# Row normalisation by absolute sums: whole 48 KB packets, a held load, and a one-row lead of the first store

## The chip, the core and the metric

The kernel runs on one core of one Trainium2 chip. The metric is device time in microseconds, the median of several executions. A second source is the profile: one execution recorded by the hardware profiler, with its own span from the first to the last instruction.

The engines that matter are VectorE (DVE in the profile), ScalarE (ACT), SyncE (SP) and the 16 DMA engines that move data between the main memory (HBM) and the on-chip buffer (SBUF). A DMA is issued by an instruction in the queue of SyncE (loads here; the profile calls the DMA queue q1) or of ScalarE (stores here; q10). Instructions of one queue run in their order, and each may first wait for semaphores, which other instructions or finished DMAs raise.

## The reference

```python
x: (32, 512, 1024) float32

def reference(x):
    sums = np.sum(np.abs(x), axis=-1, keepdims=True)
    return (x / (sums + 1e-8)).astype(np.float32)
```

There are 16,384 rows of 1,024 numbers, 4 KB each: 67.11 MB are read and 67.11 MB written. Each row is divided by the sum of its absolute values.

## The kernel before

The rows are cut into 11 tiles. Each of the 128 partitions holds 12 rows of a tile (48 KB a partition, 6,144 KB a tile), except in the last tile, which has 8 rows. `HEAD = 32` rows of a partition make up tiles 0, 1 and the last; within a partition the rows of a tile are contiguous in HBM, so a load or store may move up to 48 KB in one piece.

Four buffers of 48 KB a partition hold the tiles (`sbuf`, `BUFS = 4`): the pool gives out a buffer each time a tile is requested, and a fifth request gets the first buffer back, once all that used it is done. A tile is loaded by `load(i)` (line 87, SyncE's queue), worked on in place by `compute(i)`, and written by `store(i)` (line 97, ScalarE's queue). So the load of tile i + 4 waits for the store of tile i to have landed.

`compute(i)` calls `normalize`, which runs on VectorE: line 47 sums the absolute values of each row (a reduction over the tile), line 54 adds 1e-8, line 56 takes the reciprocal (the row factors `inv`), line 58 multiplies the first `kv` rows by their factors, and line 65 does `kt` rows one at a time. The remaining `ks` rows are scaled by ScalarE in line 68. `split` gives `(kt, ks)`: (3, 4) for tile 0, (0, 3) for tiles 1 and 2, (0, 2) for tile 9 and (4, 4) for tile 10; all others are scaled by VectorE alone.

`max_dma_last_dim` sets the piece, called a packet here, in which a DMA moves a partition's rows. Each of the 16 DMA engines serves 8 partitions. Before, tiles 0 and 1 are loaded in packets of 48 KB (`WHOLE`) and the others of 24 KB (`HALF`; the last tile's come to 16 KB). The store of tile 0 is in two parts: 3 rows in packets of 4 KB, then 9 rows in packets of 36 KB. Tile 8 is stored by two DMAs of 6 rows, tiles 9 and 10 in whole packets, the others in 24 KB packets.

The schedule is by hand (`manual_schedule`): each engine's queue has its instructions in the order in which the code calls them. The calls are load(0) to load(3), then compute(0), store(0), load(4), compute(1), store(1), load(5) and so on.

Of the kernel before, what the change touches and what calls it, by code (L numbers as in the profile page):

```python
# [1 line left out]

# [4 lines left out]

FP32 = mybir.dt.float32
EPS = 1e-8


@with_exitstack
def kernel(
    ctx: ExitStack,
    tc: tile.TileContext,
    x: bass.AP,
    out: bass.AP,
):
    nc = tc.nc
    P = nc.NUM_PARTITIONS  # L20

    x_flat = x.flatten_outer_dims()
    out_flat = out.flatten_outer_dims()
    n, d = x_flat.shape

    R = 12
    BUFS = 4
    HEAD = 32
    per_partition = n // P
    assert n % P == 0 and (per_partition - HEAD) % R == 0  # L30
    rows = [R] * ((per_partition - HEAD) // R + 2) + [HEAD - 2 * R]

    def piece(flat, i):
        head = flat[: P * HEAD, :].rearrange("(p r) d -> p r d", p=P)
        if i < 2:
            return head[:, R * i : R * (i + 1), :]
        if i == len(rows) - 1:
            return head[:, 2 * R :, :]
        a = P * (HEAD + R * (i - 2))
        return flat[a : a + P * R, :].rearrange("(p r) d -> p r d", p=P)  # L40

    sbuf = ctx.enter_context(tc.tile_pool(name="sbuf", bufs=BUFS))
    stats = ctx.enter_context(tc.tile_pool(name="stats", bufs=len(rows)))

    def normalize(x_tile, k, kv, kt):
        s = stats.tile([P, R], FP32)
        nc.vector.tensor_reduce(  # L47
            out=s[:, :k],
            in_=x_tile[:, :k, :],
            axis=mybir.AxisListType.X,  # L50
            op=mybir.AluOpType.add,
            apply_absolute_value=True,
        )
        nc.vector.tensor_scalar_add(out=s[:, :k], in0=s[:, :k], scalar1=EPS)  # L54
        inv = stats.tile([P, R], FP32)
        nc.vector.reciprocal(out=inv[:, :k], in_=s[:, :k])  # L56
        if kv:
            nc.vector.tensor_mul(  # L58
                out=x_tile[:, :kv, :],
                in0=x_tile[:, :kv, :],  # L60
                in1=inv[:, :kv].unsqueeze(2).to_broadcast([P, kv, d]),
            )
        for r in range(kv, kv + kt):
            row = x_tile[:, r, :]
            nc.vector.tensor_scalar_mul(out=row, in0=row, scalar1=inv[:, r : r + 1])  # L65
        for r in range(kv + kt, k):
            row = x_tile[:, r, :]
            nc.scalar.activation(  # L68
                out=row,
                in_=row,  # L70
                func=mybir.ActivationFunctionType.Copy,
                scale=inv[:, r : r + 1],
            )

    last = len(rows) - 1
    split = {0: (3, 4), 1: (0, 3), 2: (0, 3), last - 1: (0, 2), last: (4, 4)}

    tiles = {}

    HALF, WHOLE = 24576, 49152
    FIRST = 3

    def load(i):
        x_tile = tiles[i] = sbuf.tile([P, R, d], FP32, name="x_tile")
        nc.sync.dma_start(out=x_tile[:, : rows[i], :], in_=piece(x_flat, i), max_dma_last_dim=WHOLE if i < 2 else HALF)  # L87

    def store(i):
        if i == 0:  # L90
            parts = [(0, FIRST, 4 * d), (FIRST, R, WHOLE)]
        elif i == last - 2:
            parts = [(0, R // 2, HALF), (R // 2, R, HALF)]
        else:
            parts = [(0, rows[i], WHOLE if i >= last - 1 else HALF)]
        for a, b, size in parts:
            nc.scalar.dma_start(
                out=piece(out_flat, i)[:, a:b, :],
                in_=tiles[i][:, a:b, :],
                max_dma_last_dim=size,  # L100
            )

    def compute(i):
        k = rows[i]
        kt, ks = split.get(i, (0, 0))
        normalize(tiles[i], k, k - kt - ks, kt)

    with tc.manual_schedule():
        for i in range(BUFS):
            load(i)  # L110
        for i in range(len(rows)):
            compute(i)
            store(i)
            if i + BUFS < len(rows):
                load(i + BUFS)


# [1 line left out]
_INS = ['x']  # L119
_OUTS = [((32, 512, 1024), 'float32')]  # L120


# [23 lines left out]
```

## Time and profile before

| what | us |
|---|---|
| median of 3 runs | 316.6 (316.44 to 316.62) |
| span of the profiled execution | 315.2 |
| VectorE busy | 260.6 |
| ScalarE busy | 18.5 |
| VectorE waiting for loads | 29.8, of which 17.8 for the first |
| mean rate of the DMA engines over the span | 426 GB/s |

The profile's times are microseconds from the start of its span. In a line of the timeline the columns are start, duration, engine, line of the code and operation; in the chain of waits they are start, duration and what the chain went through; in the list of waits they are total, number of times, and longest. The lines of the kernel are those of the kernel before.

### The profile page before, as it was taken

The numbers are of one execution on the slowest core, as the hardware profiler recorded it, in microseconds if no ns is written. First come the engines' busy times: TensorE is split into PE (matmuls) and PEld (weight loads), VectorE is DVE, ScalarE is ACT, GpSimd is POOL, SyncE is SP. The second block draws the span as 40 slices with busy tenths as digits, with TensorE's granted clock in tenths as the row PEclk, the third lists the DMA queues.
The fourth block names the chain that finished last, engine by engine and source line by source line (L and its number), as shares of the span: only waits on it lengthen the run. The fifth ranks groups of instructions, "written<-read, shape, count | busy, mean of one in ns | idle before, by whom it ended". The sixth has DMA issues, their size and how long they took to land.

```text
span 315.2 us, 172 instructions
## 1 busy us (share of the span) xinstructions
DVE 260.6 (83%) x50; ACT 18.5 (6%) x17; POOL 0.2 (0%) x4
## 2 busy tenths in 40 slices
DVE  0079999999999999989996997999699969999000
ACT  0010503004000000000000000000000000203200
POOL 0000000000000000000000000000000000000000
DMA  8999999999999999999999999999999999999997
GB/s 318 480 399 412 437 407 464 411 436 413 415 446 437 415 446 437 415 449 434 415 449 437 412 449 437 412 449 437 415 446 437 415 437 434 432 428 496 399 408 324
DMA packets 5761, 134.22 MB, mean 426 GB/s; under 512 B 385, under 2 KB 385, under 8 KB 769
## 3 DMA queue, kind: packets, MB, share of 16 engines
q1 hardware_dynamic: 2736, 67.11, 49.8%
q10 hardware_dynamic: 3024, 67.11, 49.4%
q14 instruction: 1, 0.00, 0.0%
HBM read 67.11 MB, written 67.11 MB: 426 GB/s over the span
## 4 chain that ended last, share of the span: by engine, by line
DVE 40%; DMA 33%; another core or an unknown queue 18%; ACT 1%; issue 0%; SPq 0%
DVE s L47 23%; DMA x_tile<-in_x_dram 17%; DMA out_dram<-x_tile 16%; DVE x_tile L58 15%; ACT x_tile L68 1%; DVE x_tile L65 1%; DVE inv L56 0%; DVE s L54 0%; SPq L87 0%
## 5 line engine op out<-in xcount | busy, mean ns | idle before, releaser
L47 DVE TENSOR_REDUCE s<-x_tile 128x12 f32<-128x12288 f32 (+1 forms) x11 | 138.2, 12562 | 29.8 <-DMA x_tile<-in_x_dram 29.8
L58 DVE TENSOR_TENSOR x_tile<-x_tile,inv 128x12288 f32<-128x12288 f32 (+3 forms) x10 | 113.6, 11358 | 0.5
L68 ACT ACTIVATE x_tile<-x_tile,inv 128x1024 f32<-128x1024 f32 x16 | 17.2, 1138 | 256.9 <-DVE inv L56 256.9
L65 DVE TENSOR_SCALAR x_tile<-x_tile,inv 128x1024 f32<-128x1024 f32 x7 | 4.8, 749 | 0.0
L56 DVE RECIPROCAL inv<-s 128x12 f32<-128x12 f32 (+1 forms) x11 | 2.5, 226 | 0.4
L68 ACT ACT_TABLE_LOAD x1 | 1.3, 1283 | 17.8 <-DMA x_tile<-in_x_dram 17.8
L54 DVE TENSOR_SCALAR s<-s 128x12 f32<-128x12 f32 (+1 forms) x11 | 1.9, 174 | 0.4
L130 POOL MEMSET const-bfloat16-1.0<- 128x1 bf16 x1 | 0.1, 101 | 0.0
L130 POOL MEMSET const-uint8-127<- 128x1 uint8 x1 | 0.1, 101 | 0.0
L130 POOL MEMSET const-float32-0.0<- 128x1 f32 x1 | 0.1, 98 | 0.2 <-issue 0.2
L130 POOL MEMSET const-float32-1.0<- 128x1 f32 x1 | 0.1, 98 | 0.0
## 6 DMA issues: line engine op xcount, KB each, us to landing
x_tile<-in_x_dram SPq DMA_DIRECT2D x10, 6144.0 KB, 36.9
out_dram<-x_tile ACTq DMA_DIRECT2D x8, 6144.0 KB, 49.1
out_dram<-x_tile ACTq DMA_DIRECT2D x2, 3072.0 KB, 33.4
out_dram<-x_tile ACTq DMA_DIRECT2D x1, 4608.0 KB, 37.9
x_tile<-in_x_dram SPq DMA_DIRECT2D x1, 4096.0 KB, 32.2
out_dram<-x_tile ACTq DMA_DIRECT2D x1, 4096.0 KB, 20.9
out_dram<-x_tile ACTq DMA_DIRECT2D x1, 1536.0 KB, 29.3
```

Of the source, the lines that this page charges most:

```text
L47: nc.vector.tensor_reduce(out=s[:, :k], in_=x_tile[:, :k, :], axis=mybir.AxisListType.X, op=mybir.AluOpType.add, apply_absolute_value=True,)
L54: nc.vector.tensor_scalar_add(out=s[:, :k], in0=s[:, :k], scalar1=EPS)
L56: nc.vector.reciprocal(out=inv[:, :k], in_=s[:, :k])
L58: nc.vector.tensor_mul(out=x_tile[:, :kv, :], in0=x_tile[:, :kv, :], in1=inv[:, :kv].unsqueeze(2).to_broadcast([P, kv, d]),)
L65: nc.vector.tensor_scalar_mul(out=row, in0=row, scalar1=inv[:, r : r + 1])
L68: nc.scalar.activation(out=row, in_=row, func=mybir.ActivationFunctionType.Copy, scale=inv[:, r : r + 1],)
L130: nc = _bacc.Bacc("TRN2", target_bir_lowering=False, num_devices=1)
```

## The change

All loads and stores use packets of 48 KB (32 KB for the last tile), except the lead of the first store, which is now one row instead of three; the rest of that store is 11 rows in packets of 44 KB. Tile 8 is stored by one DMA.

Only tiles 0, 1 and 2 are loaded ahead of the loop (`EARLY = 3`). `load(3)` is now called from within `compute(1)`, after line 56 has made the factors of tile 1 and before its rows are multiplied. There, one number in each partition of tile 3's new buffer is first written by VectorE with a copy of a factor (`tensor_copy`, 128 x 1), and the load, which overwrites it, has to come after that copy. The loop itself is as before, with `load(i + BUFS)` at the end of step i.

```diff
-    def normalize(x_tile, k, kv, kt):
+    def normalize(x_tile, k, kv, kt, between):
...
         inv = stats.tile([P, R], FP32)
         nc.vector.reciprocal(out=inv[:, :k], in_=s[:, :k])
+        between(inv)
...
+    PACKET = 49152
+    FIRST = 1
+    EARLY = 3
...
-    HALF, WHOLE = 24576, 49152
-    FIRST = 3
-
-    def load(i):
+    def load(i, after=None):
         x_tile = tiles[i] = sbuf.tile([P, R, d], FP32, name="x_tile")
-        nc.sync.dma_start(out=x_tile[:, : rows[i], :], in_=piece(x_flat, i), max_dma_last_dim=WHOLE if i < 2 else HALF)
+        if after is not None:
+            nc.vector.tensor_copy(out=x_tile[:, 0, 0:1], in_=after[:, 0:1])
+        nc.sync.dma_start(out=x_tile[:, : rows[i], :], in_=piece(x_flat, i), max_dma_last_dim=PACKET)
 
     def store(i):
-        if i == 0:
-            parts = [(0, FIRST, 4 * d), (FIRST, R, WHOLE)]
-        elif i == last - 2:
-            parts = [(0, R // 2, HALF), (R // 2, R, HALF)]
-        else:
-            parts = [(0, rows[i], WHOLE if i >= last - 1 else HALF)]
+        k = rows[i]
+        parts = [(0, FIRST, 4 * d), (FIRST, k, PACKET)] if i == 0 else [(0, k, PACKET)]
...
     def compute(i):
         k = rows[i]
         kt, ks = split.get(i, (0, 0))
-        normalize(tiles[i], k, k - kt - ks, kt)
+
+        def between(inv):
+            if i == 1:
+                load(EARLY, after=inv)
+
+        normalize(tiles[i], k, k - kt - ks, kt, between)
 
     with tc.manual_schedule():
-        for i in range(BUFS):
+        for i in range(EARLY):
             load(i)
         for i in range(len(rows)):
             compute(i)
             store(i)
             if i + BUFS < len(rows):
                 load(i + BUFS)
```

## The prediction

> **What bounds the kernel now.** I read the page first: spans, busy shares, DMA row and queues.
>
> ```profile
> span 315.2 us, 172 instructions
> ...
> DVE 260.6 (83%) x50; ACT 18.5 (6%) x17; POOL 0.2 (0%) x4
> ...
> DMA  8999999999999999999999999999999999999997
> ...
> q1 hardware_dynamic: 2736, 67.11, 49.8%
> q10 hardware_dynamic: 3024, 67.11, 49.4%
> ```
>
> VectorE has 55 us to spare; the DMA engines have none. Their row is full in every slice but the first and last, and the two queues' packets fill 99.2% of the span. The bytes are fixed, so the time falls only if packets get cheaper, and grows by every microsecond in which both queues stand empty. Next, the list of waits of VectorE and of SyncE's queue, and the chain of waits:
>
> ```profile
> DVE s L47 <- DMA x_tile<-in_x_dram: 29.8, 6, 17.8
> ...
> SPq L87 <- DMA out_dram<-x_tile: 242.1, 8, 63.3
> ```
>
> ```profile
> 0.73 17.05 DMA x_tile<-in_x_dram
> ...
> 160.35 0.37 SPq L87
> ...
> 189.48 0.37 SPq L87
> ```
>
> SyncE's loads wait for stores to give buffers back, and one cycle of load and store takes 189.48 - 160.35 = 29.1 us. VectorE waits 29.8 - 17.8 = 12.0 us for later loads, so it has little more slack than that. Last the timeline of tiles 0 to 3, which shows what each engine could do when:
>
> ```profile
> 36.78 2.40 ACTq L97 DMA_DIRECT2D out_dram<-x_tile  x2
> ...
> 51.84 0.23 DVE L56 RECIPROCAL inv<-s 128x12 f32<-128x12 f32 x1
> 52.10 9.76 DVE L58 TENSOR_TENSOR x_tile<-x_tile,inv 128x9216 f32<-128x9216 f32 x1
> ...
> 61.78 12.94 DVE L47 TENSOR_REDUCE s<-x_tile 128x12 f32<-128x12288 f32 x1
> ...
> 84.91 12.94 DVE L47 TENSOR_REDUCE s<-x_tile 128x12 f32<-128x12288 f32 x1
> ...
> 111.23 12.95 DVE L47 TENSOR_REDUCE s<-x_tile 128x12 f32<-128x12288 f32 x1
> ...
> 293.25 0.34 ACTq L97 DMA_DIRECT2D out_dram<-x_tile  x1
> ```
>
> The second part of store 0 (9 rows) goes out at the end of the 2.40 us, near 38.8, and the page's DMA issues give it 37.9 us to land: 76.7. Until then the DMA engines carry four loads and store 0 without a hole. The last store is issued at 293.25 and ends the kernel.
>
> **The order of the loads.** The loop still calls load(4) after store(0), and that is ahead of compute(1), from which load(3) is now called. So the fourth load on SyncE is that of tile 4, not tile 3, and the fourth request to the pool is tile 4's. It takes the free fourth buffer and waits for nothing: four loads still go out at once. Tile 3 is the fifth request; it gets tile 0's buffer. Its `tensor_copy` writes that buffer, so it must wait until both parts of store 0 have read it out. In the built program VectorE's copy, between tile 1's reciprocal and its multiplication, waits for exactly these two DMAs, and SyncE's fifth load for them and for VectorE.
>
> Queued behind the copy on VectorE is everything else: the multiplication of tile 1, hence store 1 on ScalarE's queue, all later stores behind it, and load(5) on SyncE, which needs store 1. What is late next is therefore store 1.
>
> **Edit 1, packets: -1.37 us.** The trace's packet records give 912 ns for 24 KB and 1,815 ns for 48 KB, so one packet more costs 2 x 912 - 1,815 = 9 ns (a 4 KB packet's 159 ns fits: 9 plus a twelfth of 1,806). Packets per engine removed: loads of tiles 2 to 9, 16 to 8 each, 64, and the last tile 8; stores of tiles 1 to 8, 64; store 0, from 24 + 8 to 8 + 8, 16. Together 152 x 9 ns = 1.37 us, all on the DMA engines, which set the end. Bounds: 0 (nothing gained in the mixed stretches) and -1.37. I take the full amount, since the 912 ns are those of the mixed stretches.
>
> The Trainium skill (DMA: Bandwidth & Descriptors, Why small descriptors are slow) has a fixed overhead of about 3 cycles per packet and holds combining descriptors worthwhile only up to 256 B. Taken as a rule that widening 24 KB packets gives nothing, the sum would be 1.37 us higher. The rows, two sizes on both queues, speak for the small gain.
>
> **Edit 2, the lead of store 0: nothing.** One row in 4 KB packets takes turns with 8 load packets per engine instead of 24, so store 0 claims its full share earlier and tile 4's load lands later than it would behind three rows. But the four loads and store 0 are all queued, and the engines finish the five together: at 76.7 less the packets saved so far (16 of store 0, 16 of two loads, 32 x 9 ns = 0.3), 76.4. What covers it is the queued load of tile 4; without it the 16 turns less, at 0.912 + 0.159 us, would bring store 0's second part forward by 17 us.
>
> **Edit 3, the wait on VectorE.** Before, the multiplication of tile 1 began at 52.10. Now the copy begins at 76.4. It is not in the trace; the nearest rows are 128x12 operations of 0.17 (line 54) and 0.23 us (line 56), and I take 0.2; its bounds are 0 and 0.23. VectorE loses 24.5 us, of which 12.0 were waits for loads that vanish. From 52.10 to the last store's issue there were 241.2 us with those 12.0 in them, so 229.1 of work: the last store now goes out at 76.6 + 229.1 = 305.7.
>
> **First hole in the DMA.** At 76.4 store 0 has landed, and no load or store is queued. Load 3 goes out after the copy. The price of starting on empty engines is in the chain's first row: 17.05 us for load 0, against 8 packets of 1,815 ns, 14.52; 2.53 us beyond the packets. The packet records split it: 1.0 from issue to first packet, 0.74 (mean of the engines) to 1.18 (the slowest) by which the first packets are longer, some 0.3 from the last packet to the waiter. I take the middle of the stretch, 0.96, and get 0.3 + 0.06 (SyncE's wait to issue in the chain, 160.28 to 160.35) + 1.0 + 0.96 = 2.3; with the copy, 2.5. Bounds: without any stretch 1.55, with the slowest engine's and both roundings 2.8.
>
> The Trainium skill (DMA: Bandwidth & Descriptors, Anatomy of one DMA) gives a fixed cost of about 2.0 us per DMA, for transfers issued by GpSimd; no run here shows one. By that figure the two holes would be 4.2 us together and not 4.8, and the estimate 0.6 us lower.
>
> **Second hole.** Load 3 and store 1 are the DMA's next work, 2 tiles of 14.5 us from 78.9 on: they end at 107.9, as seen by a waiter 108.2. Store 1 is issued at 76.6 + 9.8 = 86.4, before load 3 alone has ended at 93.4, so the engines stay full. Then load 5, which waits for store 1, goes out at 108.2; store 2 waits for VectorE, which needs 84.91 - 61.78 = 23.1 us from 86.4: 109.5. Neither is there when the engines run dry. The hole is 2.3 us (1.35 to 2.6).
>
> **And then.** Load 5 and store 2 end near 139; store 3 is issued at 109.5 + 26.3 (111.23 - 84.91) = 135.8, some 3 us early. VectorE's cycle, 26.3 us, is shorter than the DMA's 29.1, so the lead grows and no third hole comes. At the end stores 9 and 10 are all that is left: store 9 runs until about 308, after the last store's issue at 305.7.
>
> Sum against the profiled execution: 315.2 - 1.37 + 2.5 + 2.3 = 318.6. The runs' median lies 316.6 - 315.2 = 1.4 above its span, so the forecast is **320.1 us**. With all bounds: 318.1 (holes 1.55 and 1.35) to 322.0 (holes 2.8 and 2.6, no packet gain).
>
> **The rivals.**
>
> *The change does what its words say.* Load 3 holds the fourth place on SyncE and waits only for VectorE's factors at 52.1; the copy doesn't wait for store 0. Store 0 then shares with three loads only and lands some 10 us sooner, no hole opens, and only the packets count: 316.6 - 1.4 = 315.2, faster than before. It decides if load 3's buffer is free when the copy comes up at 52.1. Against it stands the program's order. 6%.
>
> *Engines restart without a stretch.* The long first packets at 2 us may belong to the program's start. Both holes then have about 1.5 us: 318.1 to 318.6. 14%.
>
> *A third hole, or VectorE as the bound.* If store 3 comes 3 us later than worked out, a further 2.3 us go: 322.4. Or the last store comes after store 9 has ended: VectorE's chain sets the end, at 305.7 + 2.5 + 9.7 (8 packets of 1,213 ns) = 317.9, with the 1.0 from the last landing to the span's end (315.2 against 293.25 + 20.9) 318.9 and in the runs 320.3. That lies just above the DMA's own end, so each microsecond of VectorE's delay beyond the forecast is then a microsecond more. For it: VectorE is left without a wait from 76.6 on. Against: its rows vary by only 0.01 us. 18%, 321.3 to 324.
>
> The forecast as worked out holds 62%, from 318.6 to 321.3.
>
> **Range and chances.** From 318.0, just below the shortest holes, to 322.4, a third hole. About 0.2% (0.6 us) is what a measurement of this kernel tells from no change: faster 0.06, within it 0.02, slower 0.92.
>
> **What would show it.** Packets fall from 5,761 by 16 x 152 and by the 16 semaphore packets of the one DMA fewer, to 3,313. VectorE's longest idle time stands ahead of line 89 or 59, near 52 to 76, released by a store; after it VectorE waits for no load. The DMA row has two dips, near 76 and 108. Line 47 first works on the fifth-loaded tile near 109. The last store is issued near 305.7. Wrong would be: no idle time of some 24 us on VectorE (load 3 wasn't behind store 0), or that idle time with no dips (the DMA had other work).

## The result and the profile after

The changed kernel takes 325.67 us (median of 3 runs, 324.97 to 326.66) against 316.52 for the kernel before (median of 4, 316.36 to 316.62): a ratio of 1.0292, with a 95% interval of 1.027 to 1.0314. A fourth run, 330.46 us, was in the slower state that some executions fall into, and is left out here and in every comparison below (with it the median is 326.17). The forecast was slower, at 320.1 us, with 322.4 as the upper end of its range; the measured loss is about 9.2 us where 3.5 was expected. The profiled execution is the slowest of the three, 326.66 us, with a span of 324.9, 9.7 us longer than the 315.2 before.

The lines of the page that answer to those shown of the kernel before (the last two are the loads' and the stores' queue, with packets, MB and the share of the 16 engines' span that the packets took):

```profile
span 324.9 us, 172 instructions
...
DVE 260.1 (80%) x51; ACT 18.5 (6%) x17; POOL 0.2 (0%) x4
...
DMA  9999999997999999999999999999998999999994
...
q1 hardware_dynamic: 1584, 67.11, 49.2%
q10 hardware_dynamic: 1728, 67.11, 48.0%
```

These lines split the loss of the profiled execution. Before, the packets took 49.8 + 49.4 = 99.2% of 315.2 us, 312.7 us, and 2.5 us were unfilled. Now they take 97.2% of 324.9, 315.8 us, and 9.1 are unfilled. So there are 6.6 us in which engines, on average, had nothing to move, and the packets, though 152 fewer per engine, took 3.1 us longer in sum instead of 1.37 less. (The shares are rounded to 0.1%, some 0.3 us; summed from the packet records, the times are 312.9 and 315.9.)

The list of waits (total, times, longest) and the timeline show where it begins:

```profile
DVE x_tile L89 <- DMA out_dram<-x_tile: 25.0, 1, 25.0
...
DVE s L47 <- DMA x_tile<-in_x_dram: 17.7, 1, 17.7
...
SPq L90 <- DMA out_dram<-x_tile: 250.9, 8, 52.6
```

```profile
51.74 0.23 DVE L56 RECIPROCAL inv<-s 128x12 f32<-128x12 f32 x1
...
76.94 0.15 DVE L89 COPY x_tile<-inv 128x1 f32<-128x1 f32 x1 [24.97 <-DMA out_dram<-x_tile]
77.02 9.75 DVE L59 TENSOR_TENSOR x_tile<-x_tile,inv 128x9216 f32<-128x9216 f32 x1
...
86.85 0.34 ACTq L96 DMA_DIRECT2D out_dram<-x_tile  x1
...
109.97 158.35 ACTq L96 DMA_DIRECT2D out_dram<-x_tile  x7
...
305.51 0.34 ACTq L96 DMA_DIRECT2D out_dram<-x_tile  x1
```

VectorE stands for 25.0 us at the copy, and what ends it is a store. Store 1 goes out at 86.85, store 2 at 109.97. In the kernel before, store 1 went out at 61.95:

```profile
61.95 0.39 ACTq L97 DMA_DIRECT2D out_dram<-x_tile  x1
```

After that wait at the copy VectorE of the changed kernel waits for no load at all. The table of stretches (start and end, length, busy time of VectorE, ScalarE and GpSimd with their instructions, clock, share of the DMA engines, GB/s) shows what the DMA engines had, first in the kernel before and then in the changed one:

```profile
75.00:80.00 5.00, 4.96 (x2) 3.23 (x3) 0.00 (x0) 1.00 0.92 396
...
86.00:94.00 8.00, 8.00 (x1) 0.00 (x0) 0.00 (x0) 1.00 0.97 418
...
108.00:118.00 10.00, 10.00 (x2) 0.00 (x0) 0.00 (x0) 1.00 1.00 433
```

```profile
75.00:80.00 5.00, 3.06 (x2) 0.00 (x0) 0.00 (x0) 1.00 0.51 157
...
86.00:94.00 8.00, 8.00 (x2) 0.00 (x0) 0.00 (x0) 1.00 1.04 381
...
108.00:118.00 10.00, 10.00 (x2) 0.00 (x0) 0.00 (x0) 1.00 0.80 280
```

Against the steady 433 GB/s the first hole lacks 5 x (433 - 157) / 433 = 3.2 us, the second 10 x (433 - 280) / 433 = 3.5. Between them, in 86 to 94, another 8 x (433 - 381) / 433 = 1.0 us is missing although the engines count as fully busy: there store 1 starts beside load 3.

These three figures are rough, since the table counts a packet whole in the stretch in which it starts: by the same sum the kernel before, which has no hole, lacks 0.4 us in 75 to 80. The packet records allow a finer account: spread each packet's bytes evenly over its own time, and compare what both kernels have moved by a given moment, at 433 GB/s. The changed kernel is 0.2 us behind at 75 us, 3.0 at 86, 4.3 at 94 and still at 108, 7.2 at 118, and 7.3 at 300. So the first hole cost 2.8 us, the start of store 1 beside load 3 another 1.25, and the second hole 2.9. The end shows one more thing:

```profile
316.00:320.00 4.00, 0.00 (x0) 0.00 (x0) 0.00 (x0) 1.00 0.93 401
320.00:322.00 2.00, 0.00 (x0) 0.00 (x0) 0.00 (x0) 1.00 0.12 49
322.00:324.00 2.00, 0.00 (x0) 0.00 (x0) 0.00 (x0) 1.00 0.04 16
```

From 320 us on only about two of the sixteen engines, then one, still have work. By the packet records of the trace the engines finish the last store between 320.1 and 323.3 us; before, between 313.3 and 313.8. A store has landed when the slowest engine is done, so this spread is lost time too: on average the engines finish 7.3 us later than before, the slowest 9.5.

### The profile page after: what moved, and what is told of

Same layout as the page of the kernel before. It is cut to its first block, busy times and chain, and to the rows that moved or that the text cites. A ratio compares the mean times of both kernels' runs of the same rounds, so it can differ in the third digit from the quotient of the medians.

```text
span 324.9 us, 172 instructions
## 1 busy us (share of the span) xinstructions
DVE 260.1 (80%) x51; ACT 18.5 (6%) x17; POOL 0.2 (0%) x4
## 2 busy tenths in 40 slices
DMA packets 3312, 134.22 MB, mean 413 GB/s; under 512 B 368, under 2 KB 368, under 8 KB 496
## 4 chain that ended last, share of the span: by engine, by line
DVE 76%; DMA 17%; ACT 1%; issue 0%; DVEq 0%; ACTq 0%
DVE s L47 38%; DVE x_tile L59 35%; DMA out_dram<-x_tile 12%; DMA x_tile<-in_x_dram 5%; DVE x_tile L66 1%; DVE inv L56 1%; ACT x_tile L69 1%; DVE s L54 1%; DVEq L145 0%; DVE x_tile L89 0%; DVEq L59 0%; DVEq L89 0%; ACTq L96 0%
```

## The experiments

Three questions are asked in turn: whether the order of the loads or the packets make the loss, whether it comes from the holes in the DMA or from VectorE's lateness, and what a hole and a restart cost by themselves.

**Order and packets apart.** `e1` puts load 4 behind the held load, as the change is worded:

```diff
             if i == 1:
                 load(EARLY, after=inv)
+                load(BUFS)
...
-            if i + BUFS < len(rows):
+            if i > 0 and i + BUFS < len(rows):
                 load(i + BUFS)
```

> The changed kernel with one thing moved: the load of tile 4 is called right behind that of tile 3, inside compute(1), so the held load is the fourth on SyncE. Theory A (the order of the loads makes the two holes in the DMA, and all else follows): no hole, near 315.2 us, the packets' saving alone, 316.5 - 1.4. Theory B (48 KB packets themselves cost: each time a queue of large packets starts beside the other, the packets at the join are about 1 us longer, and the engines drift apart): no hole either, but the joins of store 0 and of loads 3 and 4 add 1 to 3 us: 316 to 318.

`e2` has the changed kernel's calls and the packets of the kernel before:

```diff
-    PACKET = 49152
-    FIRST = 1
+    HALF, WHOLE = 24576, 49152
+    FIRST = 3
...
-max_dma_last_dim=PACKET)
+max_dma_last_dim=WHOLE if i < 2 else HALF)
...
-        parts = [(0, FIRST, 4 * d), (FIRST, k, PACKET)] if i == 0 else [(0, k, PACKET)]
+        if i == 0:
+            parts = [(0, FIRST, 4 * d), (FIRST, R, WHOLE)]
...
```

> The changed kernel's calls (three loads ahead, load 3 with its copy inside compute(1), load 4 still ahead of it) with the packets and the three-row lead of the kernel before. Theory A: two holes of 2.5 and 2.3 us and their consequences without the packets' saving, 321 if the holes alone count, and 326 to 328 if all of the measured loss comes with the order whatever the packets. Theory B: the holes stay, but the packets at each join are stretched less and the engines stay together: 320 to 322.

`e3` has the packets of the change and the order of the kernel before:

```diff
-    EARLY = 3
+    EARLY = BUFS
...
-            if i == 1:
-                load(EARLY, after=inv)
+            pass
```

> The packets and the one-row lead of the changed kernel with the loads in the order of the kernel before, four ahead and no copy. Theory A: 315.2 us, the saving of 1.4 alone. Theory B: the saving is eaten by the longer packets where store 0 and load 4 join, and by engines drifting apart: 316 to 318.

Measured: e1 317.89 us (ratio 1.0046, 1.0031 to 1.0061), e2 325.39 (1.0276, 1.0244 to 1.0308), e3 317.58 (1.0035, 1.0021 to 1.0049), beside 316.53 for the kernel before. The order alone costs 8.9 us and the packets alone 1.05: together 9.9, against the measured 9.2, with e2's own runs from 324.08 to 326.47. With the held load in the worded place, 7.8 us of the loss are gone. So the order makes it, as theory A says, but with far more than its two holes as priced; and the packets lose instead of gaining, as theory B says, though only a microsecond. The page and the list of waits of e2 show the same dips and the same wait with the packets of the kernel before:

```profile
DMA  8999999997999799999999999999999999999996
...
q1 hardware_dynamic: 2736, 67.11, 49.5%
q10 hardware_dynamic: 3024, 67.11, 48.2%
...
DVE x_tile L89 <- DMA out_dram<-x_tile: 24.7, 1, 24.7
```

Its packets take 97.7% of 324.3 us, 316.8: 3.9 us more than the 312.9 before, by the packet records, with the very same sizes. In these records the longer ones that the kernel before doesn't have stand mostly at 78 to 82, 88 to 93 and 111 to 115 us, behind each hole and where store 1 starts beside load 3, and at 146 to 149 and 165 to 170, behind a third stretch in which the load queue is empty (142.0 to 146.6). Longer packets thus come with the restarts, with 24 KB as with 48.

**Holes or VectorE.** `g1` calls the copy and load 3 one instruction later, behind the multiplication of tile 1:

```diff
-        between(inv)
         if kv:
             nc.vector.tensor_mul(
...
             )
+        between(inv)
```

> The changed kernel with the copy and load 3 called one instruction later on VectorE, behind the multiplication of tile 1 instead of ahead of it. Tile 4 is still loaded before tile 3, and VectorE still waits at the copy for store 0, but store 1 has been issued by then. Theory H (the loss is the two stretches in which the DMA has nothing queued, and the restarts and joins that follow): no hole, 317.5 to 319, as with the packets alone. Rival V (VectorE's late work sets the end: it still loses some 15 us at the copy): 320 to 324. Rival O (tile 4 ahead of tile 3 is what costs): as the changed kernel, 325 to 327.

`g2` drops the copy (`load(EARLY)` in place of `load(EARLY, after=inv)`):

> The changed kernel without the copy: load 3 is still called after load 4 and waits on SyncE for store 0, but VectorE waits for nothing until tile 3's own sum. Theory H: no hole, since stores 1 and 2 are issued on time, 317.5 to 319. Rival V: VectorE stands idle at tile 3 for some 20 us instead of at the copy; if its lateness sets the end, 320 to 324. Rival O: 325 to 327.

Measured: g1 319.98 us (1.0100, 1.0083 to 1.0117), g2 320.43 (1.0130, 1.0109 to 1.0151), beside 316.65. One instruction's place is worth 5.7 us. VectorE still loses 15.2 us at the copy of g1, but store 1 is out by then, and both holes are gone. From the list of waits and the table of stretches of g1:

```profile
DVE x_tile L89 <- DMA out_dram<-x_tile: 15.2, 1, 15.2
```

```profile
75.00:80.00 5.00, 2.96 (x2) 0.00 (x0) 0.00 (x0) 1.00 0.98 423
108.00:118.00 10.00, 10.00 (x1) 0.00 (x0) 0.00 (x0) 1.00 1.01 437
130.00:136.00 6.00, 6.00 (x2) 0.00 (x0) 0.00 (x0) 1.00 1.09 393
136.00:142.00 6.00, 6.00 (x1) 0.00 (x0) 0.00 (x0) 1.00 0.95 369
```

Rival O is out. Theory H alone doesn't fit: both runs are 2.4 to 2.9 us above the packets-alone run, over H's 319, and at the lower edge of V's range. VectorE's lateness reaches the DMA once more, later and smaller: store 3 comes near 134, after store 2 has run out, and between 130 and 142 some 6 x (433 - 393) / 433 + 6 x (433 - 369) / 433 = 1.4 us are missing. In g2 the same happens at 166 to 176 and at 290 to 295.

**A hole by itself.** `h1` (from the kernel before) and `h2` (from the packets-alone kernel) get one hole, with VectorE left alone: ScalarE writes one number of each partition into tile 0's buffer, for which it must wait until store 0 has landed, and only then issues store 1. Load 4, which overwrites that number, goes out behind it.

```diff
             compute(i)
+            if i == 1:
+                cell = tiles[0][:, R - 1, 0:1]
+                nc.scalar.activation(out=cell, in_=tiles[1][:, 0, 0:1], func=mybir.ActivationFunctionType.Copy)
             store(i)
+            if i == 1:
+                load(BUFS)
-            if i + BUFS < len(rows):
+            if i > 0 and i + BUFS < len(rows):
                 load(i + BUFS)
```

> The kernel before, with one hole put into the DMA and VectorE left alone: a one-number write by ScalarE into the last row of tile 0's buffer, ahead of store 1, waits until store 0 has landed, so store 1 and load 4 go out together near 76.5 us onto empty DMA engines. Store 2 is issued on time. Theory H (a hole costs its idle time, the longer packets after it, and the spread between engines that it leaves): 3 to 5 us over the kernel before, 319.5 to 321.5. Rival I (only the idle time counts, 2.3 us at most as the prediction priced it): 318.0 to 318.9. Rival V (the loss of the changed kernel came from VectorE's lateness and a hole alone is made up later): within 0.6 us of the kernel before.

> The same single hole in the kernel of the packets-alone run (317.6 us). Theory H: 3 to 5 us over that run, 320.5 to 322.5. Rival I: 319 to 320. Rival V: 317 to 318.2. If 48 KB packets make a hole dearer, the difference to the packets-alone run is larger here than that of the run with the old packets to the kernel before.

Measured: h1 320.36 us (1.0118, 1.0103 to 1.0133), h2 320.47 (1.0131, 1.0100 to 1.0162), beside 316.65. One hole with a punctual VectorE costs 3.7 us in the kernel before and 2.9 in the packets-alone kernel; h1 lies in theory H's range and h2 just under it (by 0.03 us), so H holds in the main, and 48 KB packets don't make a hole dearer. The stretch of the hole in h1, and its queues:

```profile
75.00:80.00 5.00, 4.95 (x2) 3.11 (x4) 0.00 (x0) 1.00 0.54 157
```

```profile
q1 hardware_dynamic: 2736, 67.11, 49.3%
q10 hardware_dynamic: 3024, 67.11, 49.2%
```

VectorE is busy throughout (4.95 of 5 us), and the DMA lacks the same 3.2 us as in the changed kernel (2.6 by the finer account). The packets took 98.5% of 318.6 us, 313.8: some 1 us longer than before, and 4.8 instead of 2.5 us were unfilled. The engines finish the last store 1.3 us apart instead of 0.5.

**One of the two holes filled.** `i1` is the changed kernel with six rows of tile 2 on ScalarE, so that store 2 is ready in time:

```diff
-    split = {0: (3, 4), 1: (0, 3), 2: (0, 3), last - 1: (0, 2), last: (4, 4)}
+    split = {0: (3, 4), 1: (0, 3), 2: (0, 6), last - 1: (0, 2), last: (4, 4)}
```

> The changed kernel with six rows of tile 2 scaled by ScalarE instead of three, so that VectorE's multiplication of tile 2 is some 3.3 us shorter and store 2 is issued near 107 us, before store 1 has landed near 110. The first hole stays, the second is filled. Theory H (each hole costs 3 to 4 us in the end): 322 to 323.5, against 326.2 for the changed kernel. Rival V (VectorE's lateness sets the end): VectorE ends 3 us earlier as well, but with store 9 still ahead of the last store nothing is gained beyond 1 us: 325 to 326. If the holes cost only the 2.3 us that the prediction gave each, 323.5 to 324.5.

Measured: 324.75 us (323.13 to 325.66; 1.0240, 1.0208 to 1.0273), only 0.9 less than the changed kernel, with runs that overlap, so that a gain isn't even clear. The median lies in none of the three ranges, between the last one and V's; theory H's gain didn't come. The second hole is indeed smaller:

```profile
75.00:80.00 5.00, 2.81 (x2) 0.00 (x0) 0.00 (x0) 1.00 0.52 166
...
108.00:118.00 10.00, 10.00 (x1) 0.00 (x0) 0.00 (x0) 1.00 0.94 398
```

It now lacks 10 x (433 - 398) / 433 = 0.8 us instead of 3.5. But the engines finish the last store between 317.95 and 321.94 us, 4.0 us apart instead of 3.2: on average they gained 2.2 us, the slowest 1.4. And 0.8 us of what the filled hole saved went again at 135 to 141 us, where store 3 starts beside a load (the load packets there are 0.8 us longer per engine). The price of holes doesn't simply add up; which engine falls behind, and when, differs from run to run.

**A restart without a hole.** `j1` (from the packets-alone kernel) and `j2` (from the kernel before) hold store 3 back while loads keep the engines busy:

```diff
             compute(i)
+            if i == 3:
+                for r in range(46):
+                    nc.scalar.activation(out=idle, in_=idle, func=mybir.ActivationFunctionType.Copy)
             store(i)
```

> The packets-alone kernel (317.6 us) with store 3 held back on ScalarE by 46 activations on a spare tile, until some 135 to 140 us instead of 131. Loads 5 and 6 keep the DMA engines busy meanwhile, so nothing stands idle; the store queue runs dry and starts again beside running loads. Theory J (the restart of one queue beside the other costs by itself: longer packets on the engines, some 1 us, and a spread between engines): 318.6 to 321. Rival I (only idle DMA time costs): 317.0 to 318.2, as without the hold.

> The same hold in the kernel before (316.6 us). Theory J: 317.6 to 319.5. If only 48 KB packets are stretched at a restart, 316.4 to 317.2, and so too by rival I.

Measured: j1 319.28 us (1.0101, 1.0051 to 1.0150), j2 317.88 (1.0051, 1.0029 to 1.0072), beside 316.64. Store 3 was issued at 134.4 and 134.5 us. That is 1.2 us more than the kernel before with the old packets, and 1.7 more than the packets-alone run with the large ones, though the interval of j1 is wide. The times lie in theory J's ranges, at the lower end; its mechanism is hardly seen. In the profiled executions the load packets beside which store 3 starts, near 134 to 144 us, are longer by 0.1 us per engine in j2 and 0.35 in j1, not by some 1 us. Nor is it one restart: by the packet records the store queue stands empty for some 7 us until 138, and then the load queue, whose next load waits for store 3, for 7 to 8 us until 168 (j2) and 170 (j1). What a single restart costs, and where these runs lose their time, isn't shown. Both also set the spare tile to zero on VectorE at the start, while it waits for the first load.

**The packets' microsecond.** `g3` is e3 with `PACKET = 24576`; `g4` is e1 with the packets and lead of e2.

> Order of the loads as in the kernel before, one-row lead, and packets of 24 KB everywhere, so that against the run with the packets alone only the packet size differs, and against the kernel before the lead and the packets of tiles 0, 1, 9 and 10. Theory P (48 KB packets beside a running queue stretch and let single engines fall behind): the loss of the packets-alone run is gone, 316.3 to 317.0, the extra packets costing up to 0.3 us. Rival L (the shorter lead costs, by letting the second part of store 0 join earlier beside loads): 317.2 to 318.

> The order of the change's words (load 3 held until tile 1's factors, load 4 behind it) with the packets and three-row lead of the kernel before. Theory P: no loss, 316.3 to 316.9. Rival L or a cost of holding load 3 as such: 317.5 to 318.5, as the worded order had with large packets.

Measured: g3 317.29 us (1.0024, 1.0014 to 1.0033), g4 317.39 (1.0027, 1.0017 to 1.0037), beside 316.65. Both lie above theory P's bounds, g3 inside rival L's and g4 just under them. With 24 KB packets and the short lead 0.64 us of e3's 1.05 are still there, and with the old packets the worded order loses about as much. So 48 KB packets can't be the whole cause: every departure tried from the kernel before at the start costs 0.6 to 1.4 us. The profiled executions show one more pattern. With packets of mostly 24 KB the engines finish the last store 0.5 to 1.7 us apart (the kernel before, e2, g3, g4, h1, j2); with 48 KB it is 2.1 to 4.0 in six of eight kernels (the changed one, e1, e3, g1, i1, j1), 1.4 in h2 and 0.2 in g2. One execution of each doesn't make that a cause. What the three-row lead and the packets of the kernel before do right together was not settled. No version beat the kernel before.

## Why the prediction was wrong

The kernel is slower for the reason that was given, the holes behind the wrong order, but by 9.2 us and not by 3.5. Step by step:

- **The order of the loads** was read rightly: tile 4's load goes ahead of tile 3's, the copy waits for store 0, and all of VectorE stands behind it. The 25.0 us ahead of line 89 and run e1 show it; the rival that the change does what it says is out.
- **VectorE's times** held: the copy at 76.94 (forecast 76.4), 0.15 us long (0.2), store 1 at 86.85 (86.4), store 2 at 109.97 (109.5), the last store at 305.51 (305.7). No third hole came, though the load queue alone stood empty from 141.9 to 146.4 us, and VectorE doesn't set the end: the last store waits behind store 9, whose packets ran until 310.4 to 313.6 us, and h1 loses 3.7 us with VectorE on time.
- **Packets** fell to 3,312 in the record; the forecast was 3,313.
- **Edit 1** was priced at -1.37 us. The packets-alone run is 1.05 us slower. The 9 ns per packet were read rightly from the packets' durations, but the rate gains less: by the packet records the engines moved 432.7 GB/s from 145 to 255 us before and about 433.5 in e3, 0.2% or some 0.4 us over the kernel. And the sum held nothing for what the edit moves: in the packet records of e3 the load packets beside which the second part of store 0 starts are 1.0 us longer per engine (0.56 before), and the engines end 2.5 us apart (0.5 before). On average they finish 0.1 us earlier than before; the loss is that of the slowest.
- **Edit 2**, the lead at nothing, rested on the common end of the four loads and store 0. Store 0 landed at 76.83 against 76.4, so that held; but with all packets at 24 KB and the short lead the kernel still loses 0.64 us, so "nothing" isn't shown.
- **The two holes and what follows them** are where the prediction failed. Their places and causes are right; their price, 2.5 and 2.3 us, is too small. By the finer account they cost 2.8 and 2.9 us, the first at its upper bound and the second beyond its 2.6, which is 0.9 of the miss. More was put at nothing. Where store 1 starts beside load 3, the prediction says that "the engines stay full"; 1.25 us were lost there. And at the end it treats the 16 engines as one: the slowest finishes 2.5 us after their average (0.3 before), 2.2 us more. The saving of 1.37 us doesn't appear either. The trace of the kernel before had a row for such a start: the 0.56 us per engine where the second part of store 0 begins beside loads.

In sum, 0.2 us before the first hole, 2.8 and 2.9 for the holes, 1.25 for the start of store 1 and 2.2 for the slowest engine make 9.4 of the 9.7 us between the two profiled executions. This is an account of one execution; in that of e2, with the old packets, the engines lost 8.3 us on average and the slowest only 0.6 more. The runs with a single hole fit it only roughly: two holes at 2.9 to 3.7 us make 5.8 to 7.4, against 8.9 for the order alone, and i1 shows that the parts don't simply add. Why a start beside a running queue lost 1.25 us here and so little in j1 and j2, and why engines drift apart, stays open.

The Trainium skill (DMA: Bandwidth & Descriptors, Anatomy of one DMA), with its fixed cost of about 2.0 us for a DMA issued by GpSimd, would have put the holes lower still. None is issued so here, and the measured 2.9 to 3.7 us per hole decide.

## What to carry to other kernels

Where the DMA engines are full and set the end, a wait on another engine costs what it leaves unissued: ask at each wait which transfers are behind it, and whether the queues hold work until it ends. In code that calls instructions in order, a call moved into a loop body is behind everything that the loop has called before it, and takes its buffer then. An instruction that must wait for a store goes behind the work that feeds the next store: here one place later saved 5.7 us. And where transfers end with the slowest engine, look at when each engine ends, not only at their mean share.

## What was not expected of the hardware

- A queue that ran dry can cost more than its idle time. When it starts again, packets in flight on the other queue can be longer: in the changed kernel 48 KB loads of 1,815 ns reached 3,276, at 87 to 93 us, 1.25 us per engine in sum. The size of this varies: 0.1 us per engine in j2.
- The 16 engines don't stay together. In the changed kernel both queues' transfers still end within 0.9 us on all engines at 141 to 142 us, behind the second hole. Then the load queue is empty until 146.4, the next store lands over 2.9 us, and the engines remain apart to the end, where the spread is 3.2 us; each transfer lands with the slowest. A restart isn't needed for this, nor does it always do it: in e3, which has no hole, the loads' ends go from 0.8 us apart at 225 us to 2.5 at 280, and j2 ends 0.9 us apart. The runs scatter more too: 324.97 to 326.66 us against 316.36 to 316.62. Why a given engine falls behind stays open.
- The chain of waits gives VectorE 76% of the changed kernel's span, because it follows the last store back to the engine that released it. The end was set by the DMA nevertheless, as h1 and the last store's wait behind store 9 show.
